# Two transformer blocks on one core: the weights' low parts move from GpSimd to VectorE

## The chip, the cores and the metric

The kernel runs on one core of a Trainium2 chip. A core has TensorE (PE: matmuls, and PEld, its weight loads), VectorE (DVE), ScalarE (ACT), GpSimd (POOL) and SyncE (SP, which here issues the DMAs). Each engine takes its own queue of instructions in order and waits on semaphores for the others. The metric is the device time of one execution in microseconds (us), the median of several.

## The reference

Two blocks follow each other on 512 tokens of 1024 features, in fp32. The first has two layers, each with sparse attention of 8 heads (compressed, selected and window branches), stick-breaking attention of 4 heads, gates that mix the two, and a feed-forward network. The second takes 256 context tokens beside the 512, and has a layer of latent attention and a layer of gated linear attention, both modulated by vectors that come from a conditioning input. What every layer ends with is this:

```python
mixed = (gate[..., :D_MODEL] * y_nsa + gate[..., D_MODEL:] * y_sb) @ w_out
x = x + rms_norm(mixed, norm_g[1])
hf = rms_norm(x, norm_g[2])
ff = jnp.square(jax.nn.relu(hf @ w_ff1)) @ w_ff2
return x + rms_norm(ff, norm_g[3])
...
m_lat = (silu_c @ ada_w[i] + ada_b[i]).reshape(B, N_MOD, 1, D)
```

## The kernel before, in words

All matrices are kept as pairs. The high part h of a value x is x rounded to the format in which PE multiplies in one pass (`fp32r`), the low part l is x - h. A product is then three matmuls into one PSUM tile: high by high, low by high, high by low (L211 to L213 with the weights stationary, L238 to L240 with the tokens stationary). So each weight is needed as h and l, and both are made on the chip.

`wload` does that. A weight unit (mostly 8 x 256 or 4 x 512 columns on 128 partitions, 1 MB) comes in two halves into `wraw` buffers (three of them, L185). For each half ACT casts `wraw` into `wh` (L190), and then one subtraction makes `wl` (L194): on POOL, in one instruction of 1024 columns. Where `both` is set (the first weights of a stage, which are needed at once) a half is cut in two, one for DVE and one for POOL. The pools of `wh` and `wl` hold two units, so a unit is prepared while PE uses the one before it.

DVE does nearly everything else that is elementwise: low parts of activations (L166, L333, L352), the norms (L260, L287 to L289), the residual (L308: y times gain and 1/rms, L309: x plus y), squares of the hidden layer (L522, L529, L530), the sums of the second matmul over chunks (L541), the adding of earlier partial sums in the last output projection (L609), softmax maxima. POOL keeps, beside the low parts, the softmax scalings (L1047, L1764) and some sums of squares (L299).

A feed-forward network goes through 8 chunks of 512 hidden columns. Each chunk has 2 units of the first weight and 2 of the second, and PE has 4 hidden tiles and 8 output tiles to make in it. In the first block's networks the modulation weights of the second block are multiplied in the background on DVE: `ada` brings them 512 KB at a time into two `araw` buffers and sums rows into PSUM (L1378 the first, L1380 the others), 8 such steps a chunk.

The order of the instructions is made by a scheduler when the program is built: it takes, engine by engine, whatever is ready by its own estimates, the earlier in the program first. What each engine then gets is a fixed list.

Of the kernel before, what the change touches and what calls it, by code (L numbers as in the profile page):

```python
# [11 lines left out]
F32 = mybir.dt.float32  # L12
# [3 lines left out]
ALU = mybir.AluOpType  # L16
# [34 lines left out]
class Builder:  # L51
# [117 lines left out]
    def wload(self, ap, both=False, pool=None, raws=(), after=()):  # L169

        nc = self.nc
        aps = ap if isinstance(ap, list) else [ap]
        kt, n = aps[0].shape[1], sum(a.shape[2] for a in aps)
        h = self.t(pool or self.wp, [P, kt, n], F32R, tag="wh")
        l = self.t(pool or self.wp, [P, kt, n], F32R, tag="wl")
        hk = (kt + 1) // 2
        for a, b in ((0, hk), (hk, kt)):
            if a < b:
                if raws:
                    raw = raws[a > 0]  # L180
                else:
                    raw = self.t(self.wp, [P, b - a, n], F32, tag="wraw", bufs=3)
                    c = 0
                    for x in aps:
                        nc.sync.dma_start(raw[:, :, c:c + x.shape[2]], x[:, a:b])  # L185
                        c += x.shape[2]
                step = max(1, (b - a) // 2) if both else b - a
                for x in range(a, b, step):
                    z = min(b, x + step)
                    i = nc.scalar.copy(h[:, x:z], raw[:, x - a:z - a]).ins  # L190
                    for j in after:
                        self.tc.add_manual_dep(i, j.name, NOSYNC, reason="order")
                    e = nc.vector if both and x == a else nc.gpsimd
                    e.tensor_tensor(l[:, x:z], raw[:, x - a:z - a], h[:, x:z].bitcast(F32), op=ALU.subtract)  # L194
        return h, l

    def wload_turned(self, ap, w):

        nc = self.nc
        raw = self.t(self.wp, [P, 8, 64], F32, tag="wraw", bufs=3)  # L200
        nc.sync.dma_start(raw, ap)
        x = raw.rearrange("p k (a b e) -> p k a b e", a=2, b=2)
        h, lo = (o.rearrange("p k (b a e) -> p k b a e", a=2, b=2) for o in w)
        for b in range(2):
            nc.scalar.copy(h[:, :, b], x[:, :, :, b])
            nc.gpsimd.tensor_tensor(lo[:, :, b], x[:, :, :, b], h[:, :, b].bitcast(F32), op=ALU.subtract)
# [2144 lines left out]
```

## Time and profile before

| | |
|---|---|
| median of three runs | 3435.24 us (3432.82 to 3436.9) |
| the profiled execution | 3436.59 us |
| its span, first to last instruction | 3434.8 us |
| PE busy | 3264.5 us, 95% |
| DVE busy | 2136.6 us, 62% |
| ACT busy | 1511.9 us, 44% |
| POOL busy | 1172.7 us, 34% |
| HBM traffic | 334 MB, 97 GB/s |

A matmul is pipelined, so a row of PE tells from its start until its modelled end, and PE is busy in this sense whenever one follows another closely. "Idle before" an instruction is the time that its engine did nothing before it, with what ended that time behind an arrow. The chain that ended last is followed back from the last instruction: at each step to what released it or, where nothing did, to the instruction before it on the same engine.

### The profile page before, as it was taken

The numbers are of one execution on the slowest core, as the hardware profiler recorded it, in microseconds if no ns is written. First come the engines' busy times: TensorE is split into PE (matmuls) and PEld (weight loads), VectorE is DVE, ScalarE is ACT, GpSimd is POOL, SyncE is SP. The second block draws the span as 40 slices with busy tenths as digits, with TensorE's granted clock in tenths as the row PEclk, the third lists the DMA queues.
The fourth block names the chain that finished last, engine by engine and source line by source line (L and its number), as shares of the span: only waits on it lengthen the run. The fifth ranks groups of instructions, "written<-read, shape, count | busy, mean of one in ns | idle before, by whom it ended". The sixth has DMA issues, their size and how long they took to land.

```text
span 3434.8 us, 48977 instructions
## 1 busy us (share of the span) xinstructions
PE 3264.5 (95%) x18723; PEld 2825.8 (82%) x18723; DVE 2136.6 (62%) x4036; ACT 1511.9 (44%) x3323; POOL 1172.7 (34%) x688
## 2 busy tenths in 40 slices
PE   8899989999889998999999999999999899989998
PEld 8788778778878877778888879888888888878887
DVE  6855676885875567676577765333344767873445
ACT  5445544232544555432256664422222566653223
POOL 3333334444323333434422222222232222124443
PEclk8999999999999999999999999999999999999999
DMA  5212464553321245465321131121222211123332
GB/s 177 65 62 71 143 195 127 189 183 110 108 68 59 71 141 178 143 201 178 93 69 33 48 98 60 62 62 62 62 62 64 67 64 55 61 78 100 98 96 70
DMA packets 262097, 337.68 MB, mean 98 GB/s; under 512 B 17107, under 2 KB 178110, under 8 KB 261734
## 3 DMA queue, kind: packets, MB, share of 16 engines
q1 hardware_dynamic: 261862, 334.55, 31.0%
q8 instruction: 147, 2.41, 0.3%
q14 instruction: 88, 0.72, 0.1%
HBM read 305.98 MB, written 28.52 MB: 97 GB/s over the span
## 4 chain that ended last, share of the span: by engine, by line
PE 68%; DVE 17%; ACT 6%; issue 5%; DMA 3%; POOL 1%; SPq 0%; DVEq 0%; ACTq 0%; POOLq 0%
PE mm L211 15%; PE mm L213 15%; PE mm L212 15%; PE s L211 4%; PE s L212 4%; PE s L213 4%; PE s L280 2%; DMA araw<-in_ada_w_dram 2%; ACT wh L190 1%; DVE tp L1380 1%; PE tp L1065 1%; POOL wl L194 1%; DVE y L308 1%; PE mm L238 1%; PE mm L239 1%
## 5 line engine op out<-in xcount | busy, mean ns | idle before, releaser
L194 POOL TENSOR_TENSOR wl<-wraw,wh 128x1024 fp32r<-128x1024 f32 (+2 forms) x424 | 990.7, 2355 | 1748.3 <-ACT wh L190 1698.6
L211 PE MATMUL mm<-h,wh 128*128 128x512 f32 (+1 forms) x1916 | 722.6, 378 | 28.2 <-ACT h L332 8.8
L212 PE MATMUL mm<-h,wl 128*128 128x512 f32 (+1 forms) x1916 | 712.0, 372 | 0.5 <-DVE wl L194 0.4
L213 PE MATMUL mm<-h,wh 128*128 128x512 f32 (+1 forms) x1916 | 709.4, 371 | 2.1 <-DVE h L333 1.8
L190 ACT CAST wh<-wraw 128x1024 fp32r<-128x1024 f32 (+3 forms) x454 | 429.0, 967 | 493.8 <-issue 290.6
L211 PEld LDWEIGHTS mm<-h,wh 128*128 128x128 f32 x1916 | 367.6, 192 | 89.4 <-ACT h L332 9.6
L213 PEld LDWEIGHTS mm<-h,wh 128*128 128x128 f32 x1916 | 367.0, 192 | 64.0 <-DVE h L333 3.1
L212 PEld LDWEIGHTS mm<-h,wl 128*128 128x128 f32 x1916 | 368.1, 192 | 52.2 <-DVE wl L194 0.8
L529 DVE TENSOR_TENSOR t<-t 128x512 f32<-128x512 f32 (+1 forms) x140 | 173.0, 1235 | 253.1 <-ACT hid L525 252.9
L211 PE MATMUL mm<-hid,wh 128*128 128x512 f32 (+1 forms) x848 | 293.8, 346 | 11.8 <-DVE y L541 9.6
L212 PE MATMUL mm<-hid,wl 128*128 128x512 f32 (+1 forms) x848 | 290.9, 343 | 0.0
L213 PE MATMUL mm<-hid,wh 128*128 128x512 f32 (+1 forms) x848 | 290.5, 343 | 0.0
L1380 DVE SCALAR_TENSOR_TENSOR tp<-araw,sc,tp 128x512 f32<-128x512 f32 x280 | 200.5, 749 | 51.1 <-DMA araw<-in_ada_w_dram 50.0
L541 DVE TENSOR_TENSOR y<-y,mm 128x512 f32<-128x512 f32 (+1 forms) x192 | 105.4, 549 | 193.7 <-PE mm L213 193.5
L530 DVE TENSOR_TENSOR hid<-t,hid 128x512 fp32r<-128x512 f32 (+1 forms) x176 | 205.6, 1172 | 31.5 <-ACT t L527 26.3
L213 PE MATMUL s<-hid,wh 128*128 128x512 f32 (+1 forms) x560 | 208.7, 373 | 0.0
L211 PE MATMUL s<-hid,wh 128*128 128x512 f32 (+1 forms) x560 | 208.6, 373 | 0.0
L212 PE MATMUL s<-hid,wl 128*128 128x512 f32 (+1 forms) x560 | 208.2, 372 | 0.0
L525 ACT ACTIVATE hid<-t 128x512 fp32r<-128x512 f32 (+1 forms) x176 | 97.1, 554 | 241.7 <-DVE t L522 165.9
L211 PEld LDWEIGHTS mm<-hid,wh 128*128 128x128 f32 x848 | 160.0, 189 | 38.2 <-DVE y L541 6.8
L212 PEld LDWEIGHTS mm<-hid,wl 128*128 128x128 f32 x848 | 160.1, 189 | 20.9
L213 PEld LDWEIGHTS mm<-hid,wh 128*128 128x128 f32 x848 | 160.0, 189 | 21.0
(686 smaller groups left out, 7337.1 us busy)
## 6 DMA issues: line engine op xcount, KB each, us to landing
wraw<-in_w_ff_dram SPq DMA_DIRECT2D x128, 512.0 KB
wraw<-in_mlp_w_dram SPq DMA_DIRECT2D x128, 512.0 KB
araw<-in_ada_w_dram SPq DMA_DIRECT2D x96, 512.0 KB
wraw<-in_w_in_dram SPq DMA_DIRECT2D x68, 512.0 KB
raw<-in_cmp_w_dram SPq DMA_DIRECT2D x16, 512.0 KB
td<-t SPq DMA_DIRECT2D x32, 256.0 KB
h<-td SPq DMA_DIRECT2D x32, 256.0 KB
wraw<-in_w_out_dram SPq DMA_DIRECT2D x16, 512.0 KB
```

What stands on the lines that cost most here:

```text
L190: i = nc.scalar.copy(h[:, x:z], raw[:, x - a:z - a]).ins
L194: e.tensor_tensor(l[:, x:z], raw[:, x - a:z - a], h[:, x:z].bitcast(F32), op=ALU.subtract)
L211: nc.tensor.matmul(ps, wh, mh, start=first, stop=False)
L212: nc.tensor.matmul(ps, wl, mh, start=False, stop=False)
L213: nc.tensor.matmul(ps, wh, ml, start=False, stop=last)
L238: nc.tensor.matmul(ps, h[:, sl], w[0][:, k, :n], start=k == 0, stop=False)
L280: self.nc.tensor.matmul(ps, self.ones, acc, start=first, stop=last)
L525: nc.scalar.activation(h, a, AF.Square)
L529: nc.vector.tensor_tensor(a, a, a, op=ALU.mult)
L530: nc.vector.tensor_tensor(lo, a, h.bitcast(F32), op=ALU.subtract)
L541: nc.vector.tensor_tensor(y, y, ps, op=ALU.add)
L1380: nc.vector.scalar_tensor_tensor(a, raw[:, k], sc, a, op0=ALU.mult, op1=ALU.add)
```

## The change

All low parts that `wload` makes go to DVE, in pieces of 512 columns (the step is 512 divided by the columns of a k-slice, at least one slice). POOL keeps what it has beside them: the softmax scalings, some sums, and the small subtractions of `wload_turned` and of the gate weights. The casts, the DMAs and the matmuls are as before, and so are the buffers.

```diff
--- before.py
+++ after.py
@@ -190,9 +190,15 @@
                     i = nc.scalar.copy(h[:, x:z], raw[:, x - a:z - a]).ins
                     for j in after:
                         self.tc.add_manual_dep(i, j.name, NOSYNC, reason="order")
-                    e = nc.vector if both and x == a else nc.gpsimd
-                    e.tensor_tensor(l[:, x:z], raw[:, x - a:z - a], h[:, x:z].bitcast(F32), op=ALU.subtract)
+                    self.low_parts(l[:, x:z], raw[:, x - a:z - a], h[:, x:z])
         return h, l
+
+    def low_parts(self, l, raw, h):
+
+        step = max(1, 512 // l.shape[2])
+        for k in range(0, l.shape[1], step):
+            s = slice(k, min(k + step, l.shape[1]))
+            self.nc.vector.tensor_tensor(l[:, s], raw[:, s], h[:, s].bitcast(F32), op=ALU.subtract)
 
     def wload_turned(self, ap, w):
```

Lines of the kernel after stand 6 higher from `wload_turned` on: L308 is L314, L309 is L315, L541 is L547, L1380 is L1386; the new subtraction is L201. The scheduler makes new lists. DVE has 864 instructions of the subtraction where it had 46, POOL none where it had 440.

The first place is DVE in the second layer of the second block, where the last output projection ends, its residual is added (x and y, with mod the gain and ry the 1/rms), and the second half's partial sums are collected (mm in PSUM, hc the earlier ones). Before:

```order
L308 SCALAR_TENSOR_TENSOR y_5360_30098<-y_5360_30098,mod_2895_15927,ry_30278 128x256 x2
L309 TENSOR_TENSOR x_5359_30097<-x_5359_30097,y_5360_30098 128x256 x2
L308 SCALAR_TENSOR_TENSOR y_5360_30098<-y_5360_30098,mod_2895_15927,ry_30278 128x256 x2
L309 TENSOR_TENSOR x_5359_30097<-x_5359_30097,y_5360_30098 128x256 x2
L609 TENSOR_TENSOR y_5360_30098<-mm_30334,hc_29491 128x256
L308 SCALAR_TENSOR_TENSOR y_5360_30098<-y_5360_30098,mod_2895_15927,ry_30278 128x256 x2
L309 TENSOR_TENSOR x_5359_30097<-x_5359_30097,y_5360_30098 128x256 x2
```

and after, to the first subtraction that follows:

```order
L314 SCALAR_TENSOR_TENSOR y_5360_30410<-y_5360_30410,mod_2895_16125,ry_30592 128x256 x2
L315 TENSOR_TENSOR x_5359_30409<-x_5359_30409,y_5360_30410 128x256 x2
L314 SCALAR_TENSOR_TENSOR y_5360_30410<-y_5360_30410,mod_2895_16125,ry_30592 128x256 x2
L315 TENSOR_TENSOR x_5359_30409<-x_5359_30409,y_5360_30410 128x256 x2
L615 TENSOR_TENSOR y_5360_30410<-mm_30648,hc_29799 128x256
L314 SCALAR_TENSOR_TENSOR y_5360_30410<-y_5360_30410,mod_2895_16125,ry_30592 128x256 x2
L315 TENSOR_TENSOR x_5359_30409<-x_5359_30409,y_5360_30410 128x256 x2
...
L615 TENSOR_TENSOR y_5360_30410<-mm_30686,hc_30076 128x256
L615 TENSOR_TENSOR y_5360_30410<-mm_30711,hc_30196 128x256
L201 TENSOR_TENSOR wl_30771<-wraw_30772,wh_30770 128x512
```

The run of residual instructions is the same. The weights of the next stage, whose subtractions POOL made meanwhile, come on DVE only behind it (wl is the low part, wraw the weight as it came, wh the high part).

The second place is DVE in a chunk of the first layer's feed-forward network, where the sums of the modulation weights (tp in PSUM, araw the weights) go on beside the output sums (y plus mm or s, both PSUM tiles). Before:

```order
L541 TENSOR_TENSOR y_4746<-y_4746,s_6569 128x512
L1380 SCALAR_TENSOR_TENSOR tp_6665<-araw_6511,sc_718,tp_6665 128x512
L1380 SCALAR_TENSOR_TENSOR tp_6666<-araw_6511,sc_718,tp_6666 128x512
L541 TENSOR_TENSOR y_4746<-y_4746,mm_6593 128x512
L1380 SCALAR_TENSOR_TENSOR tp_6665<-araw_6667,sc_718,tp_6665 128x512
L1380 SCALAR_TENSOR_TENSOR tp_6666<-araw_6667,sc_718,tp_6666 128x512
L1380 SCALAR_TENSOR_TENSOR tp_6665<-araw_6667,sc_718,tp_6665 128x512
L541 TENSOR_TENSOR y_4746<-y_4746,s_6607 128x512
L1380 SCALAR_TENSOR_TENSOR tp_6666<-araw_6667,sc_718,tp_6666 128x512
L1380 SCALAR_TENSOR_TENSOR tp_6665<-araw_6673,sc_718,tp_6665 128x512
L1380 SCALAR_TENSOR_TENSOR tp_6666<-araw_6673,sc_718,tp_6666 128x512
L541 TENSOR_TENSOR y_4746<-y_4746,mm_6621 128x512
```

and after:

```order
L547 TENSOR_TENSOR y_4782<-y_4782,mm_6621 128x512
L201 TENSOR_TENSOR wl_6650<-wraw_6656,wh_6649 128x512 x2
L547 TENSOR_TENSOR y_4782<-y_4782,s_6635 128x512
L1386 SCALAR_TENSOR_TENSOR tp_6733<-araw_6575,sc_718,tp_6733 128x512
L1384 TENSOR_SCALAR tp_6734<-araw_6575,sc_718 128x512
L1386 SCALAR_TENSOR_TENSOR tp_6733<-araw_6735,sc_718,tp_6733 128x512
L547 TENSOR_TENSOR y_4782<-y_4782,mm_6661 128x512
L1386 SCALAR_TENSOR_TENSOR tp_6734<-araw_6575,sc_718,tp_6734 128x512
L1386 SCALAR_TENSOR_TENSOR tp_6733<-araw_6735,sc_718,tp_6733 128x512
L1386 SCALAR_TENSOR_TENSOR tp_6734<-araw_6735,sc_718,tp_6734 128x512
L547 TENSOR_TENSOR y_4782<-y_4782,s_6675 128x512
L1386 SCALAR_TENSOR_TENSOR tp_6734<-araw_6735,sc_718,tp_6734 128x512
```

Between the output sums now stand subtractions for the units to come, and sums of the modulation weights have moved back.

## Rows read from the trace of the kernel before

**Rows 1.** The page's part 1: busy us, share of the span, instructions:

```profile
PE 3264.5 (95%) x18723; PEld 2825.8 (82%) x18723; DVE 2136.6 (62%) x4036; ACT 1511.9 (44%) x3323; POOL 1172.7 (34%) x688
```

**Rows 2.** Stretches: length; busy us (instructions) by engine; PEclk, DMA share, GB/s:

```profile
0.00:530.00 530.00, 489.07 (x2891) 430.72 (x2892) 358.06 (x731) 279.96 (x643) 183.02 (x144) 0.96 0.38 118
530.00:850.00 320.00, 320.00 (x1396) 255.34 (x1396) 233.13 (x326) 100.73 (x140) 137.13 (x57) 1.00 0.49 155
850.00:1465.00 615.00, 575.56 (x3370) 496.56 (x3369) 423.49 (x802) 314.66 (x705) 219.56 (x145) 0.98 0.35 110
1715.00:2160.00 445.00, 416.71 (x2833) 378.43 (x2831) 303.78 (x734) 253.79 (x631) 123.01 (x119) 0.97 0.19 59
2640.00:3090.00 450.00, 400.42 (x2813) 368.97 (x2812) 336.10 (x855) 262.06 (x754) 113.82 (x61) 0.96 0.21 65
```

**Rows 3.** The page's part 4: chain that ended last, by engine:

```profile
PE 68%; DVE 17%; ACT 6%; issue 5%; DMA 3%; POOL 1%; SPq 0%; DVEq 0%; ACTq 0%; POOLq 0%
```

**Rows 4.** DVE in time, 668 to 685: start, us, instruction, [idle before]:

```profile
671.18 0.69 DVE L529 TENSOR_TENSOR t<-t 128x512 f32<-128x512 f32 x1 [0.70 <-ACT hid L525]
...
676.89 2.46 DVE L529 TENSOR_TENSOR t<-t 128x512 f32<-128x512 f32 x1 [0.97 <-ACT hid L525]
...
680.00 1.28 DVE L166 TENSOR_TENSOR ada<-tp,ada 128x512 fp32r<-128x512 f32 x2
```

**Rows 5.** POOL in time, 668 to 685:

```profile
676.40 2.40 POOL L194 TENSOR_TENSOR wl<-wraw,wh 128x1024 fp32r<-128x1024 f32 x1 [6.15 <-ACT wh L190]
```

**Rows 6.** DVE in time, 3024 to 3056:

```profile
3031.22 0.88 DVE L308 SCALAR_TENSOR_TENSOR y<-y,mod,ry 128x256 f32<-128x256 f32 x2
3032.02 0.75 DVE L309 TENSOR_TENSOR x<-x,y 128x256 f32<-128x256 f32 x2
3032.69 2.97 DVE L308 SCALAR_TENSOR_TENSOR y<-y,mod,ry 128x256 f32<-128x256 f32 x2
3035.58 3.42 DVE L309 TENSOR_TENSOR x<-x,y 128x256 f32<-128x256 f32 x2
...
3038.93 0.41 DVE L609 TENSOR_TENSOR y<-mm,hc 128x256 f32<-128x256 f32 x1
```

**Rows 7.** POOL in time, 3024 to 3056:

```profile
3032.88 2.50 POOL L194 TENSOR_TENSOR wl<-wraw,wh 128x1024 fp32r<-128x1024 f32 x1 [8.76 <-ACT wh L190]
...
3036.20 2.52 POOL L194 TENSOR_TENSOR wl<-wraw,wh 128x1024 fp32r<-128x1024 f32 x1
```

**Rows 8.** Who waited for whom, PE: us in total, times, longest us:

```profile
PE mm L211 <- DVE y L609: 5.1, 1, 5.1
```

**Rows 9.** Line L194 alone, by stretch: length; DVE busy, POOL busy; PEclk, DMA:

```profile
0.00:3434.80 3434.80, 43.88 (x46) 1013.48 (x440) 0.98 0.31 98
0.00:530.00 530.00, 19.15 (x20) 144.02 (x67) 0.96 0.38 118
850.00:1465.00 615.00, 19.70 (x20) 179.29 (x82) 0.98 0.35 110
1715.00:2160.00 445.00, 5.03 (x6) 62.87 (x36) 0.97 0.19 59
2640.00:3090.00 450.00, 0.00 (x0) 99.78 (x43) 0.96 0.21 65
```

**Rows 10.** Chain that ended last, its longest pieces: start, us, what:

```profile
81.08 1.37 DVE wl L194
...
3051.79 2.49 DVE y L350
```

**Rows 11.** Who waited for whom, POOL:

```profile
POOL wl L194 <- ACT wh L190: 1711.4, 223, 43.9
```

**Rows 12.** Who waited for whom, DVE:

```profile
DVE wl L194 <- ACT wh L190: 6.7, 6, 2.5
```

**Rows 13.** All engines, 602 to 786:

```profile
602.00:786.00 184.00, 184.00 (x801) 146.50 (x800) 152.38 (x224) 57.74 (x80) 78.47 (x33) 1.00 0.57 183
```

**Rows 14.** Who waited for whom, DVE, 602 to 786:

```profile
DVE tp L1380 <- DMA araw<-in_ada_w_dram: 11.9, 15, 1.6
```

## Prediction

> **What bounds the kernel now.** I read the page's busy line first, then the table by stretch, the chain that ended last, and last the instructions of single stretches on VectorE (DVE) and GpSimd (POOL). The busy line shows PE, TensorE's matmuls, at 95% of the span, DVE at 62% and POOL at 34% [rows 1]. So at most some 170 us (3434.8 - 3264.5) can come back by filling PE's idle time. The table by stretch shows where that idle time is: in the feed-forward stretch 530 to 850 us PE is busy for 320.00 of 320, while in the attention, norm and projection stretches beside it PE lacks 28 to 50 us each [rows 2]. The rest of the document calls those four the mixed stretches. What PE waits for there is mostly DVE: the chain is 68% PE, 17% DVE, 6% ScalarE (ACT), and 1% POOL [rows 3], whose work is nearly all the line that the change removes.
>
> Why DVE is slow there shows in single instructions. A product of 512 columns, both factors in SBUF, takes 0.69 us; the same line five microseconds later takes 2.46 us [rows 4], because a low part of 2.40 us began on POOL 0.5 us before it [rows 5]; the two end within 0.6 us of each other. At 3032 us two DVE instructions of line 308 take 2.97 us and two of 309 take 3.42 us, where a pair of each just before took 0.88 and 0.75 us; L609, queued behind them, starts at 3038.93 [rows 6]. POOL's low parts ran at 3032.88 and 3036.20 [rows 7], and PE stood 5.1 us for that L609 [rows 8]. So POOL's low parts cost little on POOL, but they hold DVE up.
>
> **What goes.** All 440 low parts on POOL, 1013.48 us of its 1172.7 [rows 1, 9]. DVE is no longer held by them. How much of that lies on the chain: among the 195 longest pieces of the chain, 80 are DVE pieces of over 1.1 us per instruction, 157 us in 87 instructions, the first 1.37 us at 81.08, the last 2.49 us at 3051.79 [rows 10]. Free, such an instruction (mostly 256 columns) takes 0.41 us as the L609 of rows 6 does, so 157 - 87 x 0.41 = some 120 us of holds are on the chain. Holds in shorter pieces are not in that list, so 120 is a lower end. I take 150, and 180 as the upper end; the 30 and 60 us for the unlisted ones are my assumption. POOL's own 1% of the chain, 34 us, is also replaced by pieces half as long (2 x 0.60 against 2.40 us): 15 us.
>
> **What comes.** The order of instructions holds 864 low parts on DVE where 46 stood: 818 more, of 512 columns nearly all. Two such instructions in a row take 1.28 us, one 0.68 or 0.69 [rows 4], so each adds 0.60 us: 491 us. Where they fall: in the mixed stretches POOL made 228 of them in 486.0 us [rows 9], or 202 whole ones at 2.40 us, so 405 on DVE, 243 us. The other 248 us lie in feed-forward stretches. Which share of the 243 delays the end: DVE's 17% of the chain is 584 us, and DVE is busy 358.06 + 423.49 + 303.78 + 336.10 = 1421 us in the mixed stretches [rows 2], so 41% of its work there is chain work, and I charge 100 us. The lower end is 50, because the order puts many of them off the chain: at the place of rows 6, none is left in the run of L308 and L309 (as the first pair of order rows shows). The upper end is 243, all of it.
>
> Net on the chain: 150 - 100 + 15 = 65 us. Not all of it returns, because when a DVE hold goes, ACT, PE or a transfer is next. I count three quarters, 49 us; one half and all are the ends.
>
> **Two costs beside that.** First, waiting. DVE takes its queue in order, and a low part must wait for ACT's cast. POOL stood 1711.4 us for casts in 223 waits [rows 11], which hurt nobody; DVE standing so would hurt whatever is queued behind: the norm's L308/L309, the sums of L541, the copies out of PSUM, and PE behind those. The 46 low parts that DVE makes already waited 6.7 us for their casts, 0.15 us each [rows 12]. One of the two pieces of a half can wait, 228 loads x 0.15 = 34 us, times 0.41 = 14 us; the order mostly puts them well after their casts, so I take 5. Ends 0 and 14.
>
> Second, the feed-forward network of the first layer. In 602 to 786 us DVE is busy 152.38 of 184 us with the sums of the modulation weights (L1378, L1380) beside its own work [rows 13], and the 31.6 us left include 11.9 us of waits for those weights' transfers [rows 14]. POOL's low parts there are 33 at most [rows 13], 66 x 0.60 = 40 us on DVE; held instructions give back some 7 us (one of 1.8 us in each of four chunks, as in rows 4). That makes 185 us of work for 184, and 197 if the transfers are still waited for. So DVE and PE need the same time there, and the cost lies between 1 and 13 us: I take 6. In the other feed-forward stretches DVE has room. The second pair of order rows shows the new instructions between the sums.
>
> In sum: 3436.59 (the profiled execution) - 49 + 5 + 6 = 3398.6 us. The median of the runs shown is 1.35 us below that execution, so I forecast 3397 us.
>
> **Rules weighed.** Rows 4 to 7 show that a POOL instruction which starts first holds the DVE instruction to its end. [...] Rows 4 also show two instructions of 512 columns taking 1.28 us together. [...]
>
> **Rivals.** *Holds exchanged for queueing.* DVE's new 491 us exceed anything it was held for on the chain. If the new instructions sit on the chain as thickly as the holds did, 65 us shrink to nothing: 150 + 15 - 165, with 68% instead of 41% of the 243 us on it, and the two costs remain partly: about 3436 us. For it speaks that DVE's load is hardly lower than before; against it that a hold strikes an instruction already on the chain for up to 2.4 us, whereas 0.60 us pieces leave gaps for it.
>
> *DVE stands behind the casts: slower.* One mechanism, at each load in the mixed stretches: the low part reaches the head of DVE's queue before ACT has cast, ACT itself waiting for PE to free the buffer, and the norm or softmax work behind it waits too. Each microsecond per load costs 228 x 0.41 = 93 us. It decides from 0.5 us per load (45 us, the gain); at 0.8 us the time is 3397 - 5 + 75 = 3467 us. For it speak POOL's 1711.4 us of waiting; against it the 0.15 us of rows 12.
>
> *The change doesn't bite.* If DVE is held just as long by what POOL keeps (159 us), the gain is at most 15 us minus the added work: this also ends near 3436 us or above, and I count it with the first rival.
>
> **How the numbers follow.** Forecast 0.65, own range 3350 to 3425: the best case is 180 + 15 - 50 = 145 us on the chain, of which I let half of PE's 170 us of idle time, 85 us, come back at most; the worst is half of 120 + 15 - 100 = 35, with both costs at the lower half. Holds exchanged 0.18, slower behind the casts 0.17. For a range that holds the time 8 times in 10, I go from 3345 to 3445 us. A difference under 0.2% (6.9 us) can't be told from none here. Faster: 0.65 and half of the first rival, 0.74; same 0.09, from that rival; slower 0.17.
>
> **What would show it.** Right: in the page after, L529 and L530 of 512 columns near 690 ns instead of twice that, DVE's busy time up by 50 to 200 us only (491 less the holds), POOL near 160 us, PE's idle time down by some 40 us, and the over-long DVE pieces gone from the chain. The chunk of the first layer's feed-forward between 0 and 3 us longer. Wrong: DVE waiting for ACT's cast (L190) by tens of us, or PE waiting for low parts (a wait of L212 for DVE) that it does not wait for now.

## The result, and the profile after

The kernel after takes 3334.28 us (median of 4 runs, 3330.64 to 3335.49) against 3435.58 us of the kernel before (4 runs, 3432.82 to 3436.9): 101.3 us less, a ratio of 0.9707 with a 95% interval of 0.9696 to 0.9719. The forecast was 3397 us with a range of 3345 to 3445 us, so the measured time lies below the range. Faster was right; the gain is more than twice the forecast's 38 us.

The page's busy line after, against [rows 1]:

```profile
PE 3230.7 (97%) x18723; PEld 2803.2 (84%) x18723; DVE 2231.2 (67%) x4854; ACT 1512.4 (45%) x3323; POOL 171.2 (5%) x248
```

and the chain that ended last, against [rows 3]:

```profile
PE 80%; DVE 11%; ACT 4%; issue 2%; DMA 2%; SPq 0%; DVEq 0%; ACTq 0%
```

DVE has 818 instructions more and is busy only 95 us longer (2231.2 - 2136.6), since its other instructions are no longer stretched (L529 of 512 columns took 1.21 us in the mean; the same line after, L535, takes 0.69). The chain has no POOL in it, and DVE's share fell by more than a third. PE's idle time fell from 170.3 us (3434.8 - 3264.5) to 98.2 (3328.9 - 3230.7), by 72 us. The other 34 us of the span's 106 are PE's *busy* time, with the same 18,723 matmuls. That part the prediction doesn't contain.

The stretches of [rows 2] once more, cut in the trace after where the same matmuls stand (length of the stretch; busy us and instructions by engine; granted clock, DMA share, GB/s):

```profile
0.00:497.80 497.80, 476.87 (x2891) 423.22 (x2892) 359.86 (x845) 281.56 (x644) 43.37 (x77) 0.98 0.40 125
497.80:828.50 330.70, 324.06 (x1396) 255.98 (x1396) 273.72 (x437) 100.01 (x138) 0.00 (x0) 0.99 0.48 152
828.50:1408.50 580.00, 562.99 (x3370) 490.57 (x3370) 427.11 (x942) 315.23 (x706) 44.63 (x63) 0.99 0.37 116
1655.50:2086.00 430.50, 411.64 (x2833) 373.62 (x2831) 311.02 (x786) 253.37 (x631) 62.48 (x83) 0.99 0.20 61
2566.00:2984.00 418.00, 392.78 (x2812) 363.75 (x2811) 329.01 (x939) 261.99 (x755) 15.12 (x18) 0.98 0.22 71
```

The four mixed stretches went from 2040 to 1926 us: 32, 35, 14.5 and 32 us less. The first layer's feed-forward stretch went from 320 to 330.7 us, the only one of the five that lost. In the mixed stretches PE's busy time fell from 1881.8 to 1844.3 us.

DVE at the residual, against [rows 6]:

```profile
2930.18 0.88 DVE L314 SCALAR_TENSOR_TENSOR y<-y,mod,ry 128x256 f32<-128x256 f32 x2
2930.98 0.75 DVE L315 TENSOR_TENSOR x<-x,y 128x256 f32<-128x256 f32 x2
2931.65 0.87 DVE L314 SCALAR_TENSOR_TENSOR y<-y,mod,ry 128x256 f32<-128x256 f32 x2
2932.44 0.76 DVE L315 TENSOR_TENSOR x<-x,y 128x256 f32<-128x256 f32 x2
2933.11 0.42 DVE L615 TENSOR_TENSOR y<-mm,hc 128x256 f32<-128x256 f32 x1
```

L615 starts 2.9 us after the first L314; before, L609 started 7.7 us after the first L308. PE stood 5.1 us for that L609 [rows 8]; the same wait is 0.3 us now:

```profile
PE mm L217 <- DVE y L615: 0.3, 1, 0.3
```

What the 5.1 us cost beside themselves shows in the trace of the kernel before, in stretches of 2 us (columns as above; PE is the first number behind the length, the granted clock the third from the end):

```profile
3036.00:3038.00 2.00, 0.00 (x0) 0.00 (x0) 2.00 (x2) 0.42 (x1) 2.00 (x2) 1.00 0.62 153
3038.00:3040.00 2.00, 0.61 (x3) 0.61 (x4) 2.00 (x4) 0.75 (x2) 0.79 (x2) 0.55 0.39 123
3040.00:3042.00 2.00, 2.00 (x8) 1.82 (x8) 2.00 (x6) 0.97 (x3) 0.71 (x1) 0.50 0.83 245
3042.00:3044.00 2.00, 2.00 (x7) 1.55 (x6) 1.99 (x5) 0.77 (x3) 0.78 (x1) 0.50 0.01 4
3044.00:3046.00 2.00, 2.00 (x13) 1.83 (x11) 0.49 (x2) 0.44 (x2) 0.00 (x0) 0.75 0.00 0
```

and in its matmuls of 256 columns (start, us):

```profile
3039.39 0.58 PE L211 MATMUL mm<-h,wh 128*128 128x256 f32 x1 [5.10 <-DVE y L609]
...
3040.20 0.41 PE L211 MATMUL mm<-h,wh 128*128 128x256 f32 x1
3040.41 0.41 PE L212 MATMUL mm<-h,wl 128*128 128x256 f32 x1
...
3045.07 0.28 PE L212 MATMUL mm<-h,wl 128*128 128x256 f32 x1
3045.19 0.28 PE L213 MATMUL mm<-h,wh 128*128 128x256 f32 x1
```

While PE stands for 5.1 us the granted clock falls, to 0.55 in the row from 3038 us and to 0.50 in the two from 3040 us, and it is 1.00 again from 3046 to 3048. The matmuls start 0.21 us apart at 0.50, and 0.12 us apart once the clock is back. So here the stall is paid again in slow matmuls that count as busy: from 3038.18 to 3045.01 us the clock's record is 0.50, and PE is busy for 5.62 us of that. The same order shows at the other places: in the kernel before, 26 stretches at 0.50 have matmuls in them, and in the 7 us ahead of each PE is busy for 2.8 to 5.8 us only, at a clock of 0.99 to 1.00. That the stalls are the cause is my reading of this order. At the same place after, from 2930 to 2940 us, PE lacks 1.25 us in all and the clock is 1.00:

```profile
2930.00:2940.00 10.00, 8.75 (x55) 7.34 (x54) 9.69 (x25) 7.57 (x18) 2.99 (x3) 1.00 0.00 0
```

Over the whole kernel, the clock's records in the two traces, whose only values are 0.50 and 1.00, put 115 us of PE's busy time at 0.50 before and 53 us after. Half of each is 57 and 27 us of lost work, an estimate that accounts for 31 of the 34 us.

### The profile page after: what moved, and what is told of

It is laid out like the page before. It is cut to its first block, busy times and chain, and to the rows that moved or that the text cites. A ratio compares the mean times of both kernels' runs of the same rounds, so it can differ in the third digit from the quotient of the medians.

```text
span 3328.9 us, 49257 instructions
## 1 busy us (share of the span) xinstructions
PE 3230.7 (97%) x18723; PEld 2803.2 (84%) x18723; DVE 2231.2 (67%) x4854; ACT 1512.4 (45%) x3323; POOL 171.2 (5%) x248
## 4 chain that ended last, share of the span: by engine, by line
PE 80%; DVE 11%; ACT 4%; issue 2%; DMA 2%; SPq 0%; DVEq 0%; ACTq 0%
PE mm L217 17%; PE mm L219 17%; PE mm L218 17%; PE s L218 4%; PE s L219 4%; PE s L217 4%; DVE wl L201 2%; PE s L286 2%; PE mm L244 1%; PE mm L245 1%; PE mm L246 1%; PE tp L1071 1%; ACT wh L190 1%; DVE y L314 1%; PE s L244 1%
## 5 line engine op out<-in xcount | busy, mean ns | idle before, releaser
L201 DVE TENSOR_TENSOR wl<-wraw,wh 128x512 fp32r<-128x512 f32 (+1 forms) x832 | 541.8, 684 | 302.0 <-ACT wh L190 301.2
L218 PE MATMUL mm<-h,wl 128*128 128x512 f32 (+1 forms) x1916 | 704.0, 368 | 1.4 <-DVE wl L201 1.2
L1386 DVE SCALAR_TENSOR_TENSOR tp<-araw,sc,tp 128x512 f32<-128x512 f32 x280 | 199.4, 749 | 23.2 <-DMA araw<-in_ada_w_dram 22.6
L530 ACT ACTIVATE t<-mm 128x512 f32<-128x512 f32 (+1 forms) x94 | 48.1, 512 | 263.9 <-PE mm L219 263.9
L547 DVE TENSOR_TENSOR y<-y,mm 128x512 f32<-128x512 f32 (+1 forms) x192 | 105.3, 550 | 89.1 <-PE mm L219 88.0
L535 DVE TENSOR_TENSOR t<-t 128x512 f32<-128x512 f32 (+1 forms) x140 | 89.4, 639 | 111.4 <-ACT hid L531 110.6
```

The lines of the kernel that those rows point to most:

```text
L201: self.nc.vector.tensor_tensor(l[:, s], raw[:, s], h[:, s].bitcast(F32), op=ALU.subtract)
L218: nc.tensor.matmul(ps, wl, mh, start=False, stop=False)
L530: nc.scalar.activation(a, ps, AF.Relu)
L535: nc.vector.tensor_tensor(a, a, a, op=ALU.mult)
L547: nc.vector.tensor_tensor(y, y, ps, op=ALU.add)
L1386: nc.vector.scalar_tensor_tensor(a, raw[:, k], sc, a, op0=ALU.mult, op1=ALU.add)
```

## The experiments

Each time is set against the kernel before, measured beside it: 3431.8 to 3435.6 us. On this scale the kernel after stands at -101.3 us. A hold is what [rows 4] to [rows 7] show: an instruction of DVE that starts while one of POOL runs, and doesn't end before it.

| | what | us | against before | ratio, 95% |
|---|---|---|---|---|
| E1 | no low parts | 3286.11 | -145.7 | 0.9558 to 0.9600 |
| E2 | low parts twice in the mixed stretches | 3450.79 | +19.0 | 1.0042 to 1.0072 |
| E3 | after, and holds on top | 3646.49 | +214.7 | 1.0612 to 1.0644 |
| E4 | POOL, 512 columns | 3410.95 | -20.9 | 0.9927 to 0.9957 |
| E5 | no low parts, buffers in place | 3280.97 | -152.1 | 0.9538 to 0.9566 |
| E6 | E5 with holds alone | 3424.55 | -8.5 | 0.9966 to 0.9993 |
| E7 | first layer's network on POOL | 3321.06 | -112.0 | 0.9654 to 0.9683 |
| E8 | 1024 columns on DVE | 3337.37 | -95.7 | 0.9703 to 0.9732 |
| E9 | E6 in 512 columns | 3399.88 | -33.6 | 0.9883 to 0.9916 |
| E10 | E6 with writes alone | 3280.80 | -152.6 | 0.9542 to 0.9570 |
| E11 | mixed stretches on POOL | 3444.70 | +11.3 | 1.0021 to 1.0045 |
| E12 | twice, the second aside | 3455.10 | +21.7 | 1.0046 to 1.0076 |

**What each side costs: E1, E5, E6, E10.** E1 makes a low part for the first unit only and uses it for all.

```diff
...
-        l = self.t(pool or self.wp, [P, kt, n], F32R, tag="wl")
...
+        l = made[:, :kt * n].rearrange("p (k n) -> p k n", n=n)
...
-                    self.low_parts(l[:, x:z], raw[:, x - a:z - a], h[:, x:z])
+                    if make:
+                        self.low_parts(l[:, x:z], raw[:, x - a:z - a], h[:, x:z])
```

> Only the first weight unit gets a low part; all later units use that one tile in its place (so the products lose the later weights' low parts, everything else stays). It takes away both the holds and the new work: it prices VectorE's new subtractions as (the kernel after, 3334) minus this. Theory A, as predicted (the new subtractions delay the end by about three quarters of 100 us in the mixed stretches, 5 us of waits for casts and 6 us in the first feed-forward network): 3334 - 86 = about 3250 us. Theory B (the new subtractions mostly fit into VectorE's gaps: at most the 60 us that the chain after shows for L201, of which some 70% would return, with the 10.7 us of the first feed-forward network inside it): 3290 to 3320 us.

It lay between the two. But leaving out the buffers moves the others in SBUF, and PE's busy time (3225.1 us) shows slower matmuls than E5's (3212.6), at the same mean clock of 0.994: of 512 columns, those with `h` and `wh` start 234.3 ns apart at a clock of 1.00 in E1, and 228.7 in E5, as before and after. That the places are the reason is likely, and not shown further. E5 repeats E1 with the one tile taken from the same pool, where nothing moves:

```diff
+        make = made is None or pool is not None
+        if make:
+            l = self.t(pool or self.wp, [P, kt, n], F32R, tag="wl")
```

> As the first experiment (one unit's low part stands in for all later ones), but the buffers keep the places in SBUF that they have in the kernel after: there, matmuls with h took 233 instead of 228 ns, some 17 to 25 us over the kernel, which hid part of the price. Expected where the subtractions on VectorE cost what the first experiment says plus that: 3334 - 65 = 3262 to 3275 us. Theory A (as predicted, 86 us): 3250 us. Theory B (they fit into gaps): 3290 us or more.

(38 low parts remain: the first unit's, and those of weights with buffers of their own.) Without low parts the kernel takes 152.1 us less than before. So that is what the low parts cost as they were before, nearly all of them POOL's (440, and 46 on DVE); all on DVE they cost 152.1 - 101.3 = 51 us. E5 came out between theory B and the value expected from E1.

E6 puts POOL's subtractions back into E5, into a buffer that nothing reads:

```diff
+                    else:
+                        r = raw[:, x - a:z - a]
+                        nc.gpsimd.tensor_tensor(r, r, h[:, x:z].bitcast(F32), op=ALU.subtract)
```

> The run above with GpSimd's 1024-column subtractions put back, in place in the raw weight, where nothing reads them: no low part on VectorE, nobody waits for GpSimd but the transfer into that buffer; only the holds are there. Theory 'holds are nearly all that GpSimd's low parts cost' (164 us of over-long VectorE pieces went from the chain): 120 to 160 us above the run above, 3390 to 3430 us. Rival (most of the price was that weights came late from GpSimd): 10 to 40 us above it, 3280 to 3310 us.

It is 143.6 us above E5: 94% of the 152 us, with nobody waiting for the result but a transfer. E10 replaces the subtraction in E6, which keeps the waits and the buffers as they are:

```diff
-                        nc.gpsimd.tensor_tensor(r, r, h[:, x:z].bitcast(F32), op=ALU.subtract)
+                        for _ in range(2):
+                            nc.gpsimd.memset(r, 0.0)
```

> The run with the holds alone, with two GpSimd memsets of the same 1024 columns in place of the subtraction: the same waits, the same place in GpSimd's queue and the same hold-up of the raw buffers, but GpSimd reads nothing from SBUF. Theory 'GpSimd's reading is what holds VectorE': no over-long VectorE instructions, 3281 + 0 to 10 = 3280 to 3291 us. Rival (the price is the later release of the raw buffers, or GpSimd being busy in any way): 3350 us or more.

Its page has POOL busy for 926.3 us, 79% of E6's 1177.7, and the time is E5's:

```profile
PE 3214.6 (98%) x18723; PEld 2794.9 (85%) x18723; DVE 1770.5 (54%) x4028; ACT 1509.1 (46%) x3323; POOL 926.3 (28%) x1144
```

So it isn't that POOL is busy or late, and it isn't the buffers. What the subtraction does and the memset doesn't is to read SBUF. Single instructions of E6 on DVE and POOL:

```profile
73.50 2.38 DVE L166 TENSOR_TENSOR vsp<-t,vsp 128x128 fp32r<-128x128 f32 x1 [0.41 <-ACT vsp L165]
75.81 2.38 DVE L776 TENSOR_SCALAR gates<-gates 128x24 f32<-128x24 f32 x1
```

```profile
73.35 4.79 POOL L205 TENSOR_TENSOR wraw<-wraw,wh 128x1024 f32<-128x1024 f32 x2 [5.42 <-ACT wh L198]
```

POOL's row stands for two instructions of some 2.4 us, and each of the two on DVE lasts to within 0.2 us of the end of one of them. In E10 the same two on DVE (its lines stand one lower) run while POOL writes:

```profile
70.49 0.29 DVE L166 TENSOR_TENSOR vsp<-t,vsp 128x128 fp32r<-128x128 f32 x1 [0.40 <-ACT vsp L165]
70.70 0.60 DVE L777 TENSOR_SCALAR gates<-gates 128x24 f32<-128x24 f32 x1
```

**Shorter holds: E4, E9.** E4 is the kernel before with `nc.gpsimd` in pieces of 512 columns (with it, the 46 low parts that DVE made go to POOL too):

```diff
-            self.nc.vector.tensor_tensor(l[:, s], raw[:, s], h[:, s].bitcast(F32), op=ALU.subtract)
+            self.nc.gpsimd.tensor_tensor(l[:, s], raw[:, s], h[:, s].bitcast(F32), op=ALU.subtract)
```

> All low parts stay on GpSimd, in pieces of 512 columns instead of 1024. Theory 'a VectorE instruction waits to the end of the one GpSimd instruction that runs': holds are half as long (up to 1.2 us), GpSimd's work is the same, about half of the gain comes: 3435 - 50 = 3370 to 3400 us. Rival (GpSimd starts its next piece at once and VectorE loses again, so two pieces hold as one did): 3425 to 3440 us.

It gained 21 us, between the theories, and its chain has 8% POOL, so lateness is mixed in. E9 cuts E6's subtractions in the same way, where nobody waits for them:

```diff
-                        nc.gpsimd.tensor_tensor(r, r, h[:, x:z].bitcast(F32), op=ALU.subtract)
+                        c = max(1, 512 // n)
+                        for k in range(0, z - x, c):
+                            nc.gpsimd.tensor_tensor(...)
```

> The run with the holds alone, its GpSimd subtractions cut into pieces of 512 columns: the same GpSimd work in twice as many instructions half as long, and nobody waits for it. Theory 'a VectorE instruction is held to the end of the one GpSimd instruction that runs and gets in before the next': the price of the holds, 3424.6 - 3281.0 = 143.6 us, falls by about half, 3345 to 3370 us. Rival (GpSimd's next piece starts at once and wins again): 3410 to 3430 us.

The price falls from 143.6 to 118.5 us only. The instructions of above, in E9:

```profile
74.07 1.28 DVE L166 TENSOR_TENSOR vsp<-t,vsp 128x128 fp32r<-128x128 f32 x1 [0.40 <-ACT vsp L165]
75.28 1.25 DVE L778 TENSOR_SCALAR gates<-gates 128x24 f32<-128x24 f32 x1
```

DVE does get in after one piece here, as the theory said. But the next DVE instruction meets the next piece: four pieces follow each other on POOL in 5.06 us, where two whole ones took 4.79, and a row of short DVE instructions is held one by one. So the rival's mechanism is wrong at this place, and neither number was hit.

E3 puts holds on top of the kernel after:

```diff
                     self.low_parts(l[:, x:z], raw[:, x - a:z - a], h[:, x:z])
+                    r = raw[:, x - a:z - a]
+                    nc.gpsimd.tensor_tensor(r, r, h[:, x:z].bitcast(F32), op=ALU.subtract)
```

> The kernel after, with GpSimd doing the same subtraction of 1024 columns again, in place in the raw weight, which nothing reads any more: GpSimd holds VectorE as often and as long as in the kernel before, but no engine waits for its result (only the next transfer into that buffer does). Theory 'holds': the over-long VectorE instructions are back (some 300 to 400 us in all instead of 20), and the time is 3334 + about 100 = 3420 to 3450 us. Rival (the gain came from weights being ready earlier: 2 x 0.6 us on VectorE instead of 2.4 us on GpSimd): 3335 to 3355 us.

It is 316 us above the kernel after (214.7 + 101.3), about three times what the theory gave. The chain names one reason: POOL now holds the low parts on DVE as well. L203, the subtraction, has 9% of the chain (some 330 us), where L201 has 2% after (some 70), and DVE is busy for 2803.8 us in the first 3640, where the same instructions take 2231.2 us in the whole kernel after. It tells nothing clean about the size, which is why E6 was run.

**What new work on DVE costs: E2, E12.** In E2 each low part outside the inner chunks of the feed-forward networks is made twice:

```diff
-            self.nc.vector.tensor_tensor(l[:, s], raw[:, s], h[:, s].bitcast(F32), op=ALU.subtract)
+            for _ in range(times):
+                self.nc.vector.tensor_tensor(l[:, s], raw[:, s], h[:, s].bitcast(F32), op=ALU.subtract)
```

> The kernel after, but each low part outside the inner chunks of the feed-forward networks is made twice by VectorE, the second time over the first: 416 instructions more of 512 columns, 416 x 0.60 = 250 us of VectorE's time in the mixed stretches. Theory A (41% of VectorE's work there delays the end, three quarters of that is seen): +75 us, 3410 us or more, since VectorE is fuller by then. Theory B (they fill gaps, 60 us on the chain in all): +20 to +40 us, 3355 to 3375 us.

E12 puts the second subtraction behind the first ones and into the raw weight:

```diff
+        for k in range(0, l.shape[1], step) if times > 1 else ():
+            s = slice(k, min(k + step, l.shape[1]))
+            self.nc.vector.tensor_tensor(raw[:, s], raw[:, s], h[:, s].bitcast(F32), op=ALU.subtract)
```

> The kernel after with the 416 further subtractions of the second experiment (outside the inner chunks of the feed-forward networks), but each group now stands behind the low parts of its half and writes into the raw weight, which nothing reads: VectorE has the same 250 us more to do, PE waits for none of it directly. Theory 'the first 243 us found VectorE's gaps, the next 250 us do not': +80 to +120 us, 3415 to 3455 us. Rival (the second experiment lost because each low part was ready later): +20 to +50 us, 3355 to 3385 us.

Both cost about 120 us over the kernel after (120.3 and 123.0), so it is DVE's time that counts and not a later low part. That is E12's theory, 3 us above its +80 to +120. It is more than the +75 of theory A in E2, though E1 and E5 had put the price of the first 818 subtractions nearer to B. E5, after and E12 are three steps of the same work, in the same four stretches. E5:

```profile
0.00:492.80 492.80, 476.94 (x2891) 423.98 (x2892) 299.05 (x732) 280.94 (x644) 39.17 (x77) 0.98 0.40 128
812.80:1381.40 568.60, 559.98 (x3370) 488.49 (x3369) 347.85 (x799) 314.51 (x706) 40.41 (x63) 1.00 0.38 120
1628.40:2051.20 422.80, 408.20 (x2833) 371.51 (x2831) 279.14 (x730) 253.29 (x631) 59.02 (x83) 1.00 0.20 63
2531.20:2933.40 402.20, 385.64 (x2813) 358.15 (x2812) 282.36 (x855) 261.50 (x755) 14.69 (x18) 1.00 0.23 74
```

E12:

```profile
0.00:528.90 528.90, 491.29 (x2891) 433.87 (x2892) 431.69 (x971) 282.16 (x644) 47.04 (x77) 0.95 0.37 117
862.90:1485.10 622.20, 579.69 (x3370) 502.80 (x3369) 504.46 (x1074) 315.79 (x706) 47.34 (x63) 0.96 0.35 108
1732.10:2182.50 450.40, 420.51 (x2833) 380.09 (x2831) 343.36 (x843) 253.41 (x631) 65.92 (x83) 0.97 0.19 59
2662.70:3105.90 443.20, 401.23 (x2813) 371.71 (x2812) 369.41 (x1017) 262.61 (x755) 15.30 (x18) 0.95 0.21 67
```

| mixed stretches, us | E5 | after | E12 |
|---|---|---|---|
| length | 1886 | 1926 | 2045 |
| DVE busy (share) | 1208 (64%) | 1427 (74%) | 1649 (81%) |
| cost of the step | | 40 for 219 | 118 for 222 |

The first 219 us of work cost 18% of themselves, the next 222 us 53%. A good part of the second price is paid on PE: it is busy for 1830.8, 1844.3 and 1892.7 us in the three columns, 13.5 us more in the first step and 48.4 in the second, and the granted clock falls to 0.95 to 0.97. Whether the second step is dearer because DVE's gaps are full, or because its subtractions stand in longer rows (up to 14 in a row in E12, 5 after), no run separates.

**Parts of the change: E11, E7, E8.** E11 gives DVE the low parts of the inner feed-forward chunks alone and leaves the others on POOL as before (`pl` below is then true everywhere else, but for the halves that `both` gives to DVE). E7 is the kernel after with the first layer's inner chunks on POOL (first weights of chunks 1 to 7 and second weights of chunks 0 to 6):

```diff
+        if pl:
+            self.nc.gpsimd.tensor_tensor(l, raw, h.bitcast(F32), op=ALU.subtract)
+            return
         step = max(1, 512 // l.shape[2])
...
-            w.append(self.wload(wv[:, 4 * c:4 * c + 4, u * 512:(u + 1) * 512]))
+            w.append(self.wload(wv[:, 4 * c:4 * c + 4, u * 512:(u + 1) * 512], pl=self.stage == 0 and not last))
...
```

> One part of the change alone: VectorE makes the low parts of the inner chunks of all feed-forward networks, GpSimd those of all other stages as in the kernel before. Theory (the gain lies in the mixed stretches, the feed-forward networks only lose): 3433 + 8 = 3436 to 3446 us. Rival (half the gain comes from the feed-forward networks, where most of the over-long instructions L529 and L530 were): 3380 to 3400 us.

It is 11.3 us slower than before, as the theory said. E7 puts 10.7 us of this down to the new work in the first network, so the long L529 and L530 of the inner chunks cost next to nothing: before, PE is busy there for 320.00 of 320 us ([rows 2]), 247.82 of 250 (1465 to 1715) and 479.33 of 480 (2160 to 2640).

> The kernel after, but in the inner chunks of the first layer's feed-forward network (first weights of chunks 1 to 7, second weights of chunks 0 to 6) GpSimd makes the low parts, 1024 columns at a time. Theory: the 10.7 us that this stretch lost come from VectorE being full there (153 us of 184 with the modulation sums before, and the new work on top), and PE is busy all the time where GpSimd holds VectorE: 10.7 us come back, 3322 to 3327 us. Rival (what the holds take from VectorE there is as much as the subtractions take): 3332 to 3337 us.

It is 10.7 us below the kernel after (112.0 - 101.3; the intervals of the two ratios don't touch), all that the stretch had lost, and 1 us below the theory's 3322 to 3327. The inner chunks of that network, after (PE, PEld, DVE, ACT, POOL):

```profile
570.00:759.00 189.00, 182.36 (x776) 142.61 (x775) 178.22 (x281) 55.98 (x77) 0.00 (x0) 0.99 0.56 175
```

and in E7, where PE never stands:

```profile
570.00:759.00 189.00, 189.00 (x821) 150.47 (x821) 157.15 (x232) 58.37 (x82) 81.68 (x33) 1.00 0.57 184
```

E8 makes one DVE instruction of a half:

```diff
-        step = max(1, 512 // l.shape[2])
+        step = l.shape[1]
```

> The kernel after with each half's low part in one VectorE instruction (1024 columns, mostly) instead of pieces of 512. Theory 'the pieces leave gaps': chain work queued behind a low part waits up to 1.2 us more than 0.6 us; with some 60 us of L201 on the chain now, +10 to +40 us: 3345 to 3375 us. Rival (the pieces stand back to back anyway, as the chain's 'x2' and 'x4' pieces show, and one instruction saves the start of the second, some 0.1 us in 400): 3325 to 3336 us.

Neither number was hit; 3337.37 is 1.4 us above the rival's. It lies 5.6 us above the kernel after by the medians, but the two ratios' intervals overlap, so it can't be told from it. DVE is busy for 2202.3 us in E8's first 3330, at most 29 us less than after, so the start that one instruction saves is worth at most 0.08 us for each of the 378 instructions fewer (864 - 486), an estimate. The cutting into pieces is not what made the gain.

## Why the prediction was wrong, point by point

**The bound and the mechanism** were right. E6 and E10 show it: POOL's reading holds DVE, and that is 144 of the 152 us. That the 150 us of holds on the chain come so near is partly luck. The forecast let three quarters of them return, 112 us of PE's idle time; E6 has 107 us more of idle time than E5 (171.0 against 64.4), and 37 us more of PE's busy time (3250.1 against 3212.6), which was in no term. For POOL's own pieces, counted as 15 us, 8.5 us are left.

**The step that failed most is the charge for the new work**: "41% of its work there is chain work, and I charge 100 us". With the three quarters and the 5 and 6 us, that is 86 us; measured, 51 us: 40 in the mixed stretches where 80 were charged, and 10.7 in the first feed-forward network where 6 were. The 41% sets DVE's whole time on the chain, 584 us, against its busy time in the mixed stretches alone, and some 150 of the 584 us were the holds that leave with the change. E5, which has neither the holds nor the new work, has this chain:

```profile
PE 84%; DVE 9%; ACT 4%; DMA 2%; issue 1%; SPq 0%; DVEq 0%; ACTq 0%
```

That is some 295 of 3277 us on DVE, and by the same quotient 24% of the 1208 us that DVE is busy in the mixed stretches. The 18% that the new work cost lies near that, and well under 41%; the next helping, in E12, cost 53%. The lower end, 50, which I had drawn from the order's residual place, was the better number.

**The second is the share that returns**: "I count three quarters, 49 us". POOL's side was thereby priced at three quarters of 165, 124 us, and measured 152. I held back a quarter because something else would be late next, and for idle time that was even too little: E5 has some 106 us less of it, not 124. What the sum lacks is a term for PE's busy time. I did not see that PE's stalls were paid twice here, once as idle time and once in matmuls at a clock of 0.50 (115 us of busy time before, 53 after): [rows 2] show clocks of 0.96 to 0.98 in the mixed stretches, and I let at most PE's idle time come back. After, 34 of the 106 us came out of PE's busy time; in E5 it is 52 of 158 (3264.5 - 3212.6, of 3434.8 - 3277.0).

The two make up the miss: 152 - 124 = 28 and 86 - 51 = 35 us, together 63, the difference between a gain of 101 and one of 38.

**Waiting for casts** came out between the forecast's 5 us and the rival. DVE in the mixed stretches after, one row for each:

```profile
DVE wl L201 <- ACT wh L190: 17.4, 14, 5.4
...
DVE wl L201 <- ACT wh L190: 25.9, 15, 11.4
...
DVE wl L201 <- ACT wh L190: 27.1, 8, 14.0
...
DVE wl L201 <- ACT wh L190: 13.3, 19, 2.3
```

Together 83.7 us, 0.37 us per load: more than the 0.15 I carried over, less than the 0.5 from which the slower rival decides. What it costs is inside the 40 us.

**The rules weighed.** What POOL keeps, 171.2 us, doesn't show as holds of the low parts on DVE, and a piece costs between the 0.60 us that the prediction took and the 0.69 us of a single one:

```profile
L201 DVE TENSOR_TENSOR wl<-wraw,wh 128x512 fp32r<-128x512 f32 x804 | 527.2, 689 | 297.8 <-ACT wh L190 296.9
```

Its mean of 689 ns is that of a free one [rows 4], and 527.2 us for 804 are 0.66 us each. So one piece overlaps the next by some 0.03 us in the mean (689 - 656 ns), where two in a row in [rows 4] overlap by 0.10 (2 x 0.69 - 1.28).

**The first feed-forward network** lost 10.7 us, within the ends of 1 to 13, by the reason given: with 178 of 189 us DVE is full, and E7 takes the loss away.

**The rivals.** "Holds exchanged for queueing" needed the new work to cost 165 us on the chain; it costs 51. "Doesn't bite", by which the 159 us that POOL keeps (1172.7 - 1013.5) would hold DVE just as long, is excluded by the instructions themselves: of 512 columns, L529 and L530 took 1.21 and 1.22 us in the mean before, and the same lines take 0.69 us after:

```profile
L529 DVE TENSOR_TENSOR t<-t 128x512 f32<-128x512 f32 x112 | 135.3, 1208 | 234.3 <-ACT hid L525 234.1
L530 DVE TENSOR_TENSOR hid<-t,hid 128x512 fp32r<-128x512 f32 x112 | 136.2, 1216 | 4.1 <-DVE t L529 0.5
...
L535 DVE TENSOR_TENSOR t<-t 128x512 f32<-128x512 f32 x112 | 77.1, 689 | 104.8 <-ACT hid L531 104.0
L536 DVE TENSOR_TENSOR hid<-t,hid 128x512 fp32r<-128x512 f32 x112 | 77.0, 688 | 2.6 <-DVE t L535 0.5
```

**What was to be seen** held for L529 and L530, for DVE's busy time (95 us, within 50 to 200) and for POOL (171 us). The over-long pieces are gone: among the 195 longest of the chain, 2 DVE pieces of over 1.1 us per instruction are left, 3.7 us, where 80 had 157 us. PE's idle time fell by 72 us, not 40.

Both signs of being wrong came as well, although the kernel is faster. DVE waits for casts by tens of us, the 83.7 us above, and PE waits for low parts, where L212 waited 0.4 us before:

```profile
PE mm L218 <- DVE wl L201: 6.6, 6, 2.3
```

As signs they were badly chosen: at least half of the 83.7 us cost nothing, since waits and new work together cost 40 us in the mixed stretches.

## What to carry to other kernels

In this kernel GpSimd's subtractions, which read SBUF, were paid for by VectorE (143.6 us in E6 over E5; E10's memsets, which only write, cost none: 3280.80 us against 3280.97), and there only where VectorE is on the chain: leave such work on GpSimd where TensorE is always busy (E7, the fastest here that makes every low part, 10.7 us below the kernel after), and move it where TensorE waits for VectorE. Price new work on an engine by what its chain would be without the stalls that the change removes, as a run like E5 shows, and don't carry the price on: from 64 to 74% busy, the work added to VectorE cost 18% of itself, from 74 to 81% 53%. Where a stall of TensorE goes, look for slow matmuls behind it and count them too: here they were a third of what came back (34 of 106 us).

## What the runs showed of the hardware that was not expected

The product that the prediction shows held, L529, has both factors in SBUF. E6 shows an instruction with a single input held as well: L776, a TENSOR_SCALAR of 24 columns from SBUF to SBUF, took 2.38 us. In E5, without POOL's subtractions, it is

```profile
71.02 0.17 DVE L773 TENSOR_SCALAR gates<-gates 128x24 f32<-128x24 f32 x1
```

And POOL's memset does not hold the two-input L166 of E10 (0.29 us, as in E5), but does hold the one-input L777 behind it (0.60 us, to about the end of the first of four memsets in this row):

```profile
70.32 3.87 POOL L206 MEMSET wraw<- 128x1024 f32 x4 [8.04 <-ACT wh L198]
```

What makes the difference between L166 and L777, none of these rows shows. Over the kernel, what the memsets hold is too small to see (3280.80 us in E10, 3280.97 in E5).
